# First mixer in held side stretches with its group scale applied behind the projection; loads and score banks reordered

## The chip, the cores and the metric

One core of one Trainium2 chip. The metric is device time in microseconds of one launch; the median of three timed runs of the kernel before is 1984.05 us.

## What is computed

A decoder trunk of two layers over 256 tokens of width 1024, all in float32. Each layer is a token mixer, a layer norm, a channel mixer that looks up experts by product keys (PEER), a layer norm, and a gated embedding. Layer 0's token mixer is Mamba-2 (SSD), layer 1's is causal attention with ALiBi over 16 heads (its block of 256 holds the whole sequence). The change touches both token mixers and nothing of PEER. Cut to what matters:

```python
# layer 0: SSD, 4 groups of 8 heads of 64, state 128, two chunks of 128 tokens
z, xbc, dt = split(x @ w_in);  xbc = silu(causal_depthwise_conv(xbc, conv_w, conv_b))
cb = einsum('bclgn,bcsgn->bclsg', c_in, b_in)
y_diag = einsum('bclsgr,bcsgrp->bclgrp', cb[..., None] * decay_ls, x_dt)
states = einsum('bclgn,bclgr,bclgrp->bcgrpn', b_in, decay_to_end, x_dt)
y_off = einsum('bclgn,cbgrpn,bclgr->bclgrp', c_in, prev, exp(a_cum))
gated = (y_diag + y_off + d_skip * xs).reshape(.., G, 512) * silu(z).reshape(.., G, 512)
gated = gated * rsqrt(mean(square(gated), axis=-1) + LN_EPS)     # one scale per token and group
mix = (gated.reshape(.., 2048) * norm_g) @ w_out
# layer 1: attention
q, k, v = x @ w_qkv;  logits = q @ k * Dh**-0.5 - slope * distance (causal)
mix = (softmax(logits) @ v) @ w_out
# each layer, then
x = layer_norm(alpha * x + mix);  ffn = peer_ffn(x)
x = layer_norm(alpha * x + ffn);  x = x + sigmoid(x @ ple_w_gate) * (p @ ple_w_proj)
```

## The kernel before

A tile framework orders each engine's instructions when it builds the program: by program order where inputs are ready by its own estimate, so that later work may be put ahead of earlier work that it expects to wait. `issue_after` (`self.after`) puts what is traced inside behind a given instruction of the same engine. Each engine runs its instructions in that fixed order; SP issues all weight loads in order too.

Weights come in chunks of 128x1024 float32 (512 KB). `chunk` (L116) loads one into a ring of four raw buffers; `split` (L112) makes a high half on ScalarE (L113) and the low remainder on VectorE (L114), into a ring of four; TensorE then does three products per pair of operands (`mm3`, L136: high by high, high by low, low by high). `stationary` (L140) takes a chunk as weights, 24 matmuls of 256 columns into a `mm` bank; `moving` (L153) takes it as the moving operand, 6 matmuls of 512 columns into one of four `acc` banks. All other matmuls, the side work, are plain float32 and use the two `aux` banks.

`weave(main, side)` (L38) calls the main steps in order and spreads the side steps evenly behind them; side steps go behind the load and split of the main step's chunk.

First mixer, `ssd` (L244). For each of four groups: `ssd_in` (six chunks, each with a convolution of three VectorE steps, L361), `ssd_z` (four chunks), then the scan of `ssd_mix` as side work, then `ssd_norm`, and `ssd_out` (four chunks of the output projection). The order: in 0, in 1, z 0 and 1, in 2 and out 0, in 3 and z 2, z 3, out 1, out 2, out 3 with `end_mixer`.

`ssd_mix` (L423) has ten steps: `bc` (L433), `inputs` for two token chunks (transposes of x, L444), `weights` (L439), `carry` (B is turned, L454, copied by ScalarE, L456, multiplied to the state, L458, copied, L460), and `heads` for four pairs, each 12 records of 64-column matmuls in its own `aux` bank (L472, L474) and an eviction on VectorE (L475). `ssd_norm` (L481) gates y by z (L487), squares it (ScalarE) and sums it (GpSimd, L494), sums over partitions on TensorE (L499), takes the root (L503), puts the scale on a diagonal (L506), spreads it by a matmul with ones (L512), multiplies y by gain and scale (L520) and splits it into high and low. All four groups' products accumulate in the same four `acc` banks until the layer norm adds them to 2**0.5 x (`ln_sums`, L182).

`end_mixer` (L220) does the last chunks, the layer norm and the projection of p (`project`), whose weights `ple_load` (L210) has loaded and split.

Second mixer, `moba` (L545): eight steps j over pairs of heads. `meet` does the probabilities by v of pair j-1 (L614) and the scores of pair j+1 (L621) into both `aux` banks; `softmax` evicts each of four score blocks (L590) and takes its maximum (L592), then exponentials (L597) and the normalisation (L602); `turns` transposes pair j's probabilities (L640) into the same two banks. `ple_load` for this layer stands at j == 6.

## Time and profile before

| | us |
|---|---|
| median of 3 runs | 1984.05 (1983.73 to 1985.16) |
| the profiled execution | 1985.01 |
| its span, first to last instruction | 1983.2 |
| TensorE busy | 1965.4 |
| VectorE busy | 1548.0 |
| ScalarE busy | 1134.8 |
| GpSimd busy | 129.5 |

Durations in rows are those of the profiled execution. "Idle before" is the time in which an engine did nothing ahead of an instruction, with what released it. PE is TensorE's matmuls, PEld its weight loads, DVE VectorE, ACT ScalarE, POOL GpSimd. A float32 matmul stands as two records. Records overlap a little, since instructions are pipelined.

### The profile page before, as it was taken

The page shows a single profiled execution, that of the slowest core. Times are in us where ns is not written, and L with a number is a line of the kernel's source. Part 1 is how long each engine was busy: PE and PEld are TensorE (multiplying, and loading weights), DVE is VectorE, ACT ScalarE, POOL GpSimd, SP SyncE. Part 2 cuts the span into 40 slices and gives each one's busy share as a digit, 9 for nine tenths or more (in the row PEclk, how much of TensorE's full clock was granted, in tenths as well). Part 3 has the DMA queues.
Part 4 walks back from the last instruction along what each step waited for, and adds up shares of the span by engine and source line. Part 5 has one row for each costly group of instructions (what it writes and reads, how often), then busy time and mean ns, then how long its engine had stood idle before and what let it go on. Part 6 is the DMA issues. An engine that isn't in the chain of part 4 may idle for free.

```text
span 1983.2 us, 33753 instructions
## 1 busy us (share of the span) xinstructions
PE 1965.4 (99%) x12658; PEld 1692.4 (85%) x12658; DVE 1548.0 (78%) x3044; ACT 1134.8 (57%) x1920; POOL 129.5 (7%) x156
## 2 busy tenths in 40 slices
PE   8999999999999999999999999999999999999999
PEld 8988998888888888888888899888888888888887
DVE  8787559998888998866766755899888899886675
ACT  6755456677656444455536655667755654445553
POOL 0001001111111000000000000111111100000000
PEclk9999999999999999999999999999999999999999
DMA  7446668888787545666745556888878764566671
GB/s 285 161 139 222 208 181 237 225 215 247 213 218 213 187 162 180 229 215 203 247 135 175 197 195 182 231 226 220 244 214 221 211 190 164 175 226 218 203 249 66
DMA packets 121155, 403.01 MB, mean 203 GB/s; under 512 B 13440, under 2 KB 14368, under 8 KB 119328
## 3 DMA queue, kind: packets, MB, share of 16 engines
q1 hardware_dynamic: 102560, 367.29, 56.7%
q0 software_dynamic: 18432, 33.56, 9.9%
q8 instruction: 100, 1.64, 0.3%
q14 instruction: 63, 0.52, 0.1%
HBM read 360.92 MB, written 6.32 MB: 185 GB/s over the span
## 4 chain that ended last, share of the span: by engine, by line
PE 90%; DVE 5%; ACT 3%; issue 1%; DMA 1%; POOL 0%; SPq 0%; ACTq 0%; DVEq 0%; POOLq 0%
PE acc L138 41%; PE acc L149 22%; PE acc L150 11%; PE mm L138 10%; PE aux L895 3%; DVE hl L114 2%; ACT hl L113 1%; PE aux L743 1%; PE mm L388 1%; PE aux L472 0%; DVE act L779 0%; DVE act L780 0%; PE mm L173 0%; DMA raw<-in_w_xbc 0%; DVE act L782 0%
## 5 line engine op out<-in xcount | busy, mean ns | idle before, releaser
L114 DVE TENSOR_TENSOR hl<-raw,hl 128x1024 fp32r<-128x1024 f32 x626 | 760.8, 1221 | 245.6 <-ACT hl L113 244.1
L149 PE MATMUL acc<-xT,hl 128*128 128x512 f32 x2048 | 722.9, 397 | 0.0
L138 PE MATMUL acc<-hl,w 128*128 128x512 f32 x3024 | 695.4, 390 | 0.0
L113 ACT CAST hl<-raw 128x1024 fp32r<-128x1024 f32 x626 | 658.3, 1054 | 36.3 <-PE acc L138 15.8
L138 PEld LDWEIGHTS acc<-hl,w 128*128 128x128 f32 x3024 | 565.1, 188 | 116.7
L150 PE MATMUL acc<-xT,hl 128*128 128x256 f32 x2048 | 573.3, 280 | 0.4 <-DVE hl L114 0.4
L149 PEld LDWEIGHTS acc<-xT,hl 128*128 128x128 f32 x2048 | 384.4, 188 | 89.8
L150 PEld LDWEIGHTS acc<-xT,hl 128*128 128x128 f32 x2048 | 386.5, 189 | 1.1 <-DVE hl L114 1.1
L113 ACT CAST w<-act 128x256 fp32r<-128x256 f32 x252 | 102.2, 407 | 344.6 <-PE acc L138 344.6
L138 PE MATMUL mm<-xT,hl 128*128 128x256 f32 x1968 | 252.7, 286 | 1.9 <-DVE hl L114 0.8
L138 PEld LDWEIGHTS mm<-xT,hl 128*128 128x128 f32 x1968 | 240.3, 191 | 7.9 <-issue 4.0
L861 ACT COPY act<-acc 128x256 f32<-128x256 f32 x256 | 96.3, 376 | 254.5 <-PE acc L150 254.5
L114 DVE TENSOR_TENSOR w<-act,w 128x256 fp32r<-128x256 f32 x252 | 106.8, 424 | 78.6 <-ACT w L113 78.4
L865 POOL DMA_DIRECT2D act<-low x128 | 111.1, 868 | 758.8 <-ACT low L862 629.6
L902 DVE SCALAR_TENSOR_TENSOR act<-aux,act 128x256 f32<-128x256 f32 x256 | 90.7, 417 | 9.9 <-PE aux L895 9.9
L862 ACT COPY low<-acc 128x256 f32<-128x256 f32 x256 | 98.1, 383 | 0.0
L886 DVE TENSOR_TENSOR a<-oh,r 128x512 f16<-128x512 f16 x256 | 96.6, 419 | 0.0
L880 DVE TENSOR_TENSOR oh<-iota,r 128x1024 f16<-128x1024 f16 x128 | 87.6, 684 | 0.0
L895 PEld LDWEIGHTS <-oh 128*128 128x128 f16 x2048 | 63.3, 98 | 13.4 <-issue 13.4
L895 PE MATMUL aux<-a,oh 128*128 128x64 f16 x2048 | 70.9, 193 | 0.0
L852 ACT ACTIVATE act<-act 128x1024 f32<-128x1024 f32 x64 | 69.0, 1078 | 0.8 <-DMA act<-low 0.8
L197 POOL TENSOR_TENSOR ln_s<-ln_s,mhalf 128x1 f32<-128x1 f32 x8 | 4.4, 548 | 898.0 <-DVE ln_s L196 763.5
(214 smaller groups left out, 1276.6 us busy)
## 6 DMA issues: line engine op xcount, KB each, us to landing
raw<-in_u SPq DMA_DIRECT2D x256, 512.0 KB, 4.3
raw<-in_v SPq DMA_DIRECT2D x256, 512.0 KB, 4.3
act<-low POOLq DMA_DIRECT2D x128, 256.0 KB, 5.5
raw<-in_w_q SPq DMA_DIRECT2D x32, 512.0 KB, 4.1
raw<-in_w_xbc SPq DMA_DIRECT2D x24, 512.0 KB, 4.3
raw<-in_w_z SPq DMA_DIRECT2D x16, 512.0 KB, 3.3
raw<-in_w_so SPq DMA_DIRECT2D x16, 512.0 KB, 3.8
raw<-in_w_pg SPq DMA_DIRECT2D x16, 512.0 KB, 4.7
```

The source lines that it names most:

```text
L113: a = self.nc.scalar.copy(hi, src)
L114: b = self.nc.vector.tensor_tensor(lo, src, hi.bitcast(F32), op=OP.subtract)
L138: self.last_mm = self.nc.tensor.matmul(out, lhs(a), rhs(b), start=start and i == 0, stop=stop and i == 2).ins
L149: self.nc.tensor.matmul(o, hl[:, 0, c], self.xT[:, :, k, :], start=k == 0, stop=False)
L150: self.nc.tensor.matmul(out[:, :T], hl[:, 1, c], self.xT[:, 0, k, :], start=False, stop=k == KD - 1)
L861: nc.scalar.copy(act[e // 32][:, e % 32, :], pe[:, :T])
L862: copied = nc.scalar.copy(cur["low"][:, e % 2, :], pe[:, T:]).ins
L865: nc.gpsimd.dma_start(both, cur["low"], accum_op=OP.add)
L880: nc.vector.tensor_tensor(pairs(oh2), every(self.iota, P), twins(i2T, P), op=OP.is_equal)
L886: nc.vector.tensor_tensor(pairs(a2[:, k]), pairs(oh1), twins(g2[:, k], 64), op=OP.mult)
L895: nc.tensor.matmul(pg[:, t, :], oh2[:, t], a2[:, k, t], start=k == 0, stop=k == 1)
L902: nc.vector.scalar_tensor_tensor(v, pg[:, :, 32 * a:32 * a + 32].rearrange("p t e -> p e t"), 2.0 ** -12, v, op0=OP.mult, op1=OP.mult)
```

## The change

In the first mixer, the scan's steps per group become `enter` (C by B, B turned, sums of squares of the group before, first token chunk of x turned), `weights`, a pause, `carry` (state, second token chunk turned), `weights`, `decayed`, a pause, and `heads` with all four pairs in the two `aux` banks. The matmuls of each of these three side stretches are put behind the last weight matmul issued. The group's scale is no longer spread: y times gain is split at the gate, each group has its own accumulation in the `acc` banks, and VectorE adds the result times the scale (one value per partition) to x, which is loaded during out 0 and scaled by ScalarE. For the last group the layer norm's addition does it. Group 3's scan moves from z 3 to out 1, and the loads of gain and shift and of the per-layer weights move from out 2 and behind it to z 3. `pr` is allotted in `end_mixer`.

In the second mixer, the four score evictions stand ahead of the four maxima, `ple_load` stands at j == 1, and the first scores stand behind the whole of query 1's chunk.

```diff
-    def ln_sums(self, tb, acc, x, dump, pool):
+    def ln_sums(self, tb, acc, x, dump, pool, scales=None):
...
-            nc.vector.scalar_tensor_tensor(v, v, ALPHA, acc[h], op0=OP.mult, op1=OP.add, accum_out=sm[:, h:h + 1])
+            a, scale, b = (v, ALPHA, acc[h]) if scales is None else (acc[h], scales[:, tb:tb + 1], v)
+            nc.vector.scalar_tensor_tensor(v, a, scale, b, op0=OP.mult, op1=OP.add, accum_out=sm[:, h:h + 1])
...
-        self.pr = pool.tile([P, 2, D], F32, tag="ac", bufs=4, name="pr")
...
-                self.moving(accs[tb][h], hl, lhs(kp, tb), False, final)
+                first = scales is not None and not any(h == q[0] for q in last[:n])
+                self.moving(accs[tb][h], hl, lhs(kp, tb), first, final)
...
-        sums = [self.ln_sums(tb, accs[tb], x, dump, pool) for tb in range(2)]
+        sums = [self.ln_sums(tb, accs[tb], x, dump, pool, scales) for tb in range(2)]
...
+        self.pr = pool.tile([P, 2, D], F32, tag="ac", bufs=4, name="pr")
...
-            self.weave(zs[0] + zs[1], seg[2] + exp[:1] + seg[3] + ssm[0][:6] + exp[1:] + ssm[0][6:])
+            self.weave(zs[0] + zs[1], seg[2] + exp[:1] + seg[3] + ssm[0][:7] + exp[1:] + ssm[0][7:])
             self.ssd_silu(0)
             self.ssd_silu(1)
-            self.oacc = self.accs()
-            self.weave(ins[2] + out[0], norm[0] + ssm[1])
+            def load():
+                nc.sync.dma_start(x, dram["x"].rearrange("(b p) d -> p b d", p=P))
+                for tb in range(2):
+                    nc.scalar.activation(x[:, tb], x[:, tb], AF.Copy, scale=ALPHA)
+
+            def roots():
+                pq = self.aux()
...
+                    self.ssd_sums(3, pq)
...
+            self.weave(ins[2] + out[0], norm[0] + ssm[1][:4] + [load] + ssm[1][4:])
             self.weave(ins[3] + zs[2], norm[1] + ssm[2])
             self.ssd_silu(2)
-            self.weave(zs[3], ssm[3][:6])
+            gb = pool.tile([P, 2, D], F32, tag="ac", bufs=4, name="gb")
+            self.weave(zs[3], [lambda: self.load_gb(gb, 0), lambda: self.ple_load(0, pool)])
             self.ssd_silu(3)
-            load = lambda: nc.sync.dma_start(x, dram["x"].rearrange("(b p) d -> p b d", p=P))
-            self.weave(out[1], ssm[3][6:] + norm[2] + [load])
-            gb = pool.tile([P, 2, D], F32, tag="ac", bufs=4, name="gb")
-            self.weave(out[2], norm[3] + [lambda: self.load_gb(gb, 0)])
-            self.ple_load(0, pool)
+            self.weave(out[1], norm[2] + ssm[3])
+            self.weave(out[2], norm[3] + [roots])
             self.weave(out[3], [])
             dump = pool.tile([P, D], F32, tag="y", bufs=2, name="dump")
             self.end_mixer(0, self.oacc, x, gb, dump, pool, self.last,
-                           lambda kp, tb: lambda a, k: self.ns[kp // 2][:, a, 2 * (kp % 2) + k, tb * P:(tb + 1) * P])
+                           lambda kp, tb: lambda a, k: self.ns[3][:, a, 2 * kp + k, tb * P:(tb + 1) * P], self.rs[3])
...
+        def enter():
...
+            p, px = self.aux(), self.aux()
+            with self.after((self.last_mm,)):
+                for c in range(2):
+                    sl = slice(c * P, (c + 1) * P)
+                    nc.tensor.matmul(p[:, sl], v["bf"][:, sl], v["cf"][:, sl], start=True, stop=True)
+                nc.tensor.transpose(p[:, T:T + P], v["bf"][:, :P], self.ident)
+                if g:
+                    self.ssd_sums(g - 1, p[:, 384:388])
+                turn(px, 0)
+            if g:
+                self.ssd_root(g - 1, p[:, 384:388])
+            v["bn"] = self.tl([P, P], "bn", 1)
+            nc.scalar.copy(v["bn"], p[:, T:T + P])
+            v["xe"] = scaled(px, "xe", 1, self.dtd[:, hs, None])
+            v["x", 0] = scaled(px, "xd", 4, self.dt[:, 0, hs, None])
             v["cb"] = self.tl([P, 2, P], "cbm", 2)
...
-            pb = self.aux()
...
-            pst = self.aux()
-            nc.tensor.matmul(pst, bn, v["xe"].rearrange("p h q -> p (h q)"), start=True, stop=True)
+            px, pst = self.aux(), self.aux()
+            with self.after((self.last_mm,)):
+                nc.tensor.matmul(pst, v["bn"], v["xe"].rearrange("p h q -> p (h q)"), start=True, stop=True)
+                turn(px, 1)
+            v["x", 1] = scaled(px, "xd", 4, self.dt[:, 1, hs, None])
             v["st"] = self.tl([P, 512], "st", 2)
             nc.scalar.copy(v["st"], pst)
+
+        def decayed():
...
             ce = self.ce[g]
             nc.vector.tensor_tensor(ce, ce, v["cf"][:, None, P:].to_broadcast([P, 8, P]), op=OP.mult)
...
-        def heads(j):
...
-            py = self.aux()[:, :T].rearrange("p (c l) -> p c l", c=2)
...
+        def heads():
+            y = self.ys[g] = self.tl([P, 4, T], "y", 2)
+            py = [self.aux().rearrange("p (j c l) -> p j c l", j=2, c=2) for _ in range(2)]
+            lanes = lambda j: [(2 * j + k, py[j // 2][64 * k:64 * k + 64, j % 2]) for k in range(2)]
+            with self.after((self.last_mm,)):
+                for j in range(4):
+                    for c in range(2):
+                        for h, o in lanes(j):
+                            nc.tensor.matmul(o[:, c], v["x", c][:, h, :], self.ac[g][:, h, c, :], start=True, stop=c == 0)
+                    for h, o in lanes(j):
+                        nc.tensor.matmul(o[:, 1], v["st"][:, 64 * h:64 * h + 64], self.ce[g][:, h, :], start=False, stop=True)
+            for j in range(4):
+                nc.vector.scalar_tensor_tensor(y[:, j, :], v["xs"][:, j, :], prm[:, P_D + 4 * g + j:P_D + 4 * g + j + 1],
+                                               py[j // 2][:, j % 2].rearrange("p c l -> p (c l)"), op0=OP.mult, op1=OP.add)
+
+        return [enter, lambda: weights(0), None, carry, lambda: weights(1), decayed, None, heads]
...
+                self.ns[g] = self.tl([P, 2, 4, T], "nhl", 2, F32R)
+                self.sq[g] = self.tl([P, T], "sq", 2)
+                nc.scalar.activation(self.sq[g], y, AF.Square)
...
-                nc.gpsimd.tensor_tensor(v["sq"], v["sq"], t, op=OP.add)
...
-        def scale():
-            pq = self.aux()
-            for tb in range(2):
-                nc.tensor.matmul(pq[:, 2 * tb:2 * tb + 2], v["sq"][:, tb * P:(tb + 1) * P], self.ones[:, :2],
-                                 start=True, stop=True)
-            rs = self.tl([P, 2], "rs", 2)
-            nc.vector.tensor_scalar(rs, pq[:, 0:4:2], 1.0 / 512, LN_EPS, op0=OP.mult, op1=OP.add)
-            nc.gpsimd.tensor_tensor(rs, rs, self.mhalf, op=OP.pow)
-            dg = self.tl([P, 2, P], "dg", 1)
-            for tb in range(2):
-                nc.vector.tensor_scalar(dg[:, tb, :], self.ident, rs[:, tb:tb + 1], None, op0=OP.mult)
-            v["dg"] = dg
-
-        def spread():
-            pr = self.aux()
-            dg = v["dg"]
-            nc.tensor.matmul(pr[:, :T], self.ones, dg.rearrange("p b t -> p (b t)"), start=True, stop=True)
-            v["rs"] = self.tl([P, T], "rsb", 2)
-            nc.scalar.copy(v["rs"], pr[:, :T])
-            self.ns[g] = self.tl([P, 2, 4, T], "nhl", 2, F32R)
-
-        def apply(j):
-            y, n = self.ys[g][:, j, :], self.ns[g]
-            c = 4 * g + j
-            nc.vector.scalar_tensor_tensor(y, y, prm[:, P_NG + c:P_NG + c + 1], v["rs"], op0=OP.mult, op1=OP.mult)
-            self.split(n[:, 0, j, :], n[:, 1, j, :], y)
-
-        return [lambda j=j: gate(j) for j in range(4)] + [None, scale, spread] + [lambda j=j: apply(j) for j in range(4)]
-
-    def ssd_out(self, g):
+                nc.gpsimd.tensor_tensor(self.sq[g], self.sq[g], t, op=OP.add)
+            n, gain = self.ns[g], prm[:, P_NG + 4 * g + j:P_NG + 4 * g + j + 1]
+            hi = n[:, 0, j, :]
+            nc.scalar.activation(hi, y, AF.Identity, scale=gain)
+            nc.vector.scalar_tensor_tensor(n[:, 1, j, :], y, gain, hi.bitcast(F32), op0=OP.mult, op1=OP.subtract)
+
+        return [lambda j=j: gate(j) for j in range(4)]
...
+    def ssd_sums(self, g, pq):
+        for tb in range(2):
+            self.nc.tensor.matmul(pq[:, 2 * tb:2 * tb + 2], self.sq[g][:, tb * P:(tb + 1) * P], self.ones[:, :2],
+                                  start=True, stop=True)
...
+            if kp + h == 0:
+                self.oacc = self.accs()
...
-                self.last.append((h, 2 * g + kp, hl, (0, 1)))
+                self.last.append((h, kp, hl, (0, 1)))
...
             for tb in range(2):
-                self.moving(self.oacc[tb][h], hl,
-                            lambda a, k: self.ns[g][:, a, 2 * kp + k, tb * P:(tb + 1) * P], g == 0 and kp == 0, False)
+                acc = self.oacc[tb][h]
+                self.moving(acc, hl, lambda a, k: self.ns[g][:, a, 2 * kp + k, tb * P:(tb + 1) * P], kp == 0, kp == 1)
+                if kp:
+                    v = x[:, tb, h * 512:(h + 1) * 512]
+                    self.nc.vector.scalar_tensor_tensor(v, acc, self.rs[g][:, tb:tb + 1], v, op0=OP.mult, op1=OP.add)
...
-                        nc.vector.tensor_reduce(mx[:, h2, tb:tb + 1], lg[:, h2, tb, :w], AX, OP.max)
+                for h2 in range(2):
+                    for tb in range(2):
+                        nc.vector.tensor_reduce(mx[:, h2, tb:tb + 1], lg[:, h2, tb, :(tb + 1) * P], AX, OP.max)
...
-            met = meet(None, 0)
-            with self.after(met):
-                q(1)
+            q(1)
+            meet(None, 0)
...
-                if j == 6:
+                if j == 1:
                     self.ple_load(1, pool)
```

## Rows read from the trace of the kernel before

**Rows 1.** The page: engines' busy time, then costliest groups (busy, mean ns | idle before).
```profile
PE 1965.4 (99%) x12658; PEld 1692.4 (85%) x12658; DVE 1548.0 (78%) x3044; ACT 1134.8 (57%) x1920; POOL 129.5 (7%) x156
...
L114 DVE TENSOR_TENSOR hl<-raw,hl 128x1024 fp32r<-128x1024 f32 x626 | 760.8, 1221 | 245.6 <-ACT hl L113 244.1
...
L113 ACT CAST hl<-raw 128x1024 fp32r<-128x1024 f32 x626 | 658.3, 1054 | 36.3 <-PE acc L138 15.8
```
**Rows 2.** Table by stage: window, then us and count for PE, PEld, DVE, ACT, POOL, clock, DMA.
```profile
0.00:216.00 216.00, 207.22 (x1446) 181.61 (x1446) 171.48 (x349) 136.44 (x232) 15.11 (x22) 1.00 0.58 199
...
1025.00:1160.00 135.00, 131.00 (x886) 112.32 (x884) 86.38 (x180) 77.43 (x171) 1.08 (x2) 1.00 0.48 165
```
**Rows 3.** The same table on a finer grid, one stretch of the convolutions.
```profile
125.00:145.00 20.00, 19.89 (x166) 19.64 (x165) 19.12 (x36) 13.26 (x28) 0.71 (x1) 1.00 0.35 112
```
**Rows 4.** The chain that ended last, first mixer: start us, us, what.
```profile
92.45 0.43 PE aux L512 x2
...
147.45 1.02 PE mm L138 x7
...
148.84 2.10 PE mm L138 x16
...
156.73 2.88 PE mm L138 x24
```
**Rows 5.** TensorE's waits, 0 to 216 us: total, times, longest.
```profile
PE aux L474 <- ACT st L460: 1.1, 1, 1.1
...
PE aux L458 <- ACT bn L456: 0.8, 2, 0.6
...
PE aux L512 <- DVE dg L506: 0.7, 1, 0.7
```
**Rows 6.** VectorE's groups by form, 55 to 216 us.
```profile
L520 DVE SCALAR_TENSOR_TENSOR y<-y,params,rsb 128x256 f32<-128x256 f32 x16 | 7.3, 480 | 0.1
...
L114 DVE TENSOR_TENSOR nhl<-y,nhl 128x256 fp32r<-128x256 f32 x16 | 6.4, 420 | 0.0
...
L182 DVE SCALAR_TENSOR_TENSOR xn<-xn,acc 128x512 f32<-128x512 f32 x4 | 2.7, 686 | 2.0 <-PE acc L138 2.0
...
L506 DVE TENSOR_SCALAR dg<-ident,rs 128x128 f32<-128x128 f32 x8 | 2.1, 283 | 3.1 <-POOL rs L503 3.1
```
**Rows 7.** DMA issues by tile, 100 to 216 us: size, median us to landing.
```profile
xn<-in_x SPq DMA_DIRECT2D x1, 1024.0 KB, 7.3
...
gb<-in_ln SPq DMA_DIRECT2D x1, 1024.0 KB, 6.5
```
**Rows 8.** TensorE's waits, 990 to 1170 us.
```profile
PE aux L640 <- DVE lg L590: 2.6, 3, 1.1
...
PE aux L640 <- ACT pt L644: 0.6, 1, 0.6
...
PE aux L621 <- ACT k L575: 0.5, 1, 0.5
```
**Rows 9.** Timelines in the second mixer: VectorE, TensorE, ScalarE (start us, us).
```profile
1084.58 0.61 DVE L592 TENSOR_REDUCE mx<-lg 128x1 f32<-128x256 f32 x2
...
1085.10 0.41 DVE L590 SCALAR_TENSOR_TENSOR lg<-alibi,aux 128x256 f32<-128x256 f32 x1
...
1085.58 0.82 PE L640 MATMUL aux<-ident,lg 128*128 128x128 f32 x6
...
1114.08 0.62 ACT L113 CAST pT<-raw 128x512 fp32r<-128x512 f32 x1 [3.46 <-DMA raw<-in_pT]
...
1121.54 1.22 DVE L114 TENSOR_TENSOR ppw<-raw,ppw 128x1024 fp32r<-128x1024 f32 x1
...
1125.15 0.52 PE L640 MATMUL aux<-ident,lg 128*128 128x128 f32 x3 [0.95 <-DVE lg L590]
```
**Rows 10.** Timeline of GpSimd, first mixer, two of its sums of squares.
```profile
119.03 2.37 POOL L494 TENSOR_TENSOR sq<-sq,sqt 128x256 f32<-128x256 f32 x3 [28.35 <-ACT sqt L493]
...
164.97 3.36 POOL L494 TENSOR_TENSOR sq<-sq,sqt 128x256 f32<-128x256 f32 x3 [37.47 <-ACT sqt L493]
```

More of the change, by code (lines that the diff above doesn't have):

```diff
@@ L217, in ple_load, with end_mixer @@
         self.ppw = [self.chunk(self.dram["w_pp"][i, h], hl=tile()) for h in range(2)]
-        self.pr = pool.tile([P, 2, D], F32, tag="ac", bufs=4, name="pr")
-    def end_mixer(self, i, accs, x, gb, dump, pool, last, lhs):
+    def end_mixer(self, i, accs, x, gb, dump, pool, last, lhs, scales=None):
         for tb in range(2):
@@ L262, in ssd @@
             x = pool.tile([P, 2, D], F32, name="xn")
-            self.grp, self.zs, self.ns, self.ys, self.ac, self.ce = ({} for _ in range(6))
+            self.grp, self.zs, self.ns, self.ys, self.ac, self.ce, self.sq, self.rs = ({} for _ in range(8))
             self.last = []
@@ L268, in ssd @@
             norm = [self.ssd_norm(g) for g in range(4)]
-            out = [self.ssd_out(g) for g in range(4)]
+            out = [self.ssd_out(g, x) for g in range(4)]
             seg = [[lambda g=g, c=c, k=k: self.ssd_seg(g, c, slice(4 * k, 4 * k + 4)) for c in range(2) for k in range(2)]
@@ L478, in ssd_mix @@
-        return [bc, lambda: inputs(0), lambda: weights(0), lambda: inputs(1), lambda: weights(1), carry] + [
-            lambda j=j: heads(j) for j in range(4)]
+        def heads():
+            y = self.ys[g] = self.tl([P, 4, T], "y", 2)
+            py = [self.aux().rearrange("p (j c l) -> p j c l", j=2, c=2) for _ in range(2)]
+            lanes = lambda j: [(2 * j + k, py[j // 2][64 * k:64 * k + 64, j % 2]) for k in range(2)]
+            with self.after((self.last_mm,)):
+                for j in range(4):
[4 more added lines that the diff above has]
+                        nc.tensor.matmul(o[:, 1], v["st"][:, 64 * h:64 * h + 64], self.ce[g][:, h, :], start=False, stop=True)
+            for j in range(4):
+                nc.vector.scalar_tensor_tensor(y[:, j, :], v["xs"][:, j, :], prm[:, P_D + 4 * g + j:P_D + 4 * g + j + 1],
+                                               py[j // 2][:, j % 2].rearrange("p c l -> p (c l)"), op0=OP.mult, op1=OP.add)
@@ new lines, in ssd_norm, with ssd_root @@
+        return [lambda j=j: gate(j) for j in range(4)]
[3 more added lines that the diff above has]
+                                  start=True, stop=True)
+    def ssd_root(self, g, pq):
+        nc = self.nc
+        rs = self.rs[g] = self.tl([P, 2], "rs", 2)
+        nc.vector.tensor_scalar(rs, pq[:, 0:4:2], 1.0 / 512, LN_EPS, op0=OP.mult, op1=OP.add)
+        nc.gpsimd.tensor_tensor(rs, rs, self.mhalf, op=OP.pow)
```

43 lines of the change are left out of this document (10 added, 33 removed).

## The prediction

> **What bounds the kernel now.** I first read the page for the busiest engine. TensorE is busy for 1965.4 us, 99% of the span [rows 1], so only removed matmul time, or one of the few waits in front of a matmul, can move the end. Next I read the table by stage. The first mixer (0 to 216 us) leaves TensorE idle for 8.8 us and the second (1025 to 1160 us) for 4.0 us [rows 2]; the reader should see that these two hold 12.8 of the span's 17.8 us of TensorE idle time (part of it the first load of all), and they are what the change touches. The same table on a finer grid shows the second engine at risk: in 125 to 145 us VectorE is busy 19.12 of 20 us [rows 3], because it writes the low half of each weight chunk. A VectorE edit there is not free.
>
> The profiled execution took 1985.01 us, a span of 1983.2 and 1.8 around it. It is 1.0 us above the median of the three timed runs (1984.05), so I make the sum on 1985.01 and take 1.0 off at the end. A measurement of this kernel can tell about 0.2% (4 us) from no change.
>
> **Removed in the first mixer: the spread of the scale.** Before, each group's scale per token is put on a diagonal and multiplied by ones, to stand along the free axis, before the output projection. Now it is one number per partition that multiplies the projection's result. In the chain one spread holds TensorE for 0.43 us [rows 4], and there are four: 4 x 0.43 = 1.7 us, all on the path, as TensorE does nothing else meanwhile.
>
> **Removed there: waits that sit in front of side matmuls.** The table of TensorE's waits lists 1.1 us for the state copy (line 460), 0.8 us for the copy of turned B (line 456) and 0.7 us for the diagonal (line 506) [rows 5]: 2.6 us. The diagonal is gone. The copy of B is now made in `enter`, three steps ahead of `carry`, which reads it, and the state copy four steps ahead of `heads`; a step is a chunk of 2.9 us [rows 4] or longer. The cover is that distance. If ScalarE sits behind a late transfer, the old price returns. What is late next after these is the weight chunk itself, by VectorE's splits.
>
> **Removed there: breaks in a weight chunk.** Before, the first head pair of a group cut into a chunk of 24 matmuls. In group 2 its two pieces took 1.02 + 2.10 = 3.12 us, and an uncut chunk 2.88 us [rows 4]: 0.24 us lost. Groups 1 and 2 are cut like this, group 3 once: 2.5 x 0.24 = 0.6 us. In group 0 I count nothing: there the head pairs stand while ScalarE is still working off its exponentials, so the weight chunk behind them would not be ready earlier.
>
> **Added there.** VectorE loses 16 gain multiplications (0.48 us each), 16 low halves of 0.42 and 8 diagonals of 0.28 [rows 6], by mean durations 7.7 + 6.7 + 2.3 = 16.7 us. It gains 16 low halves with the gain in them (the nearest row is the gain multiplication, 0.48) and 12 evictions of 512 columns that scale and add (nearest, the layer norm's addition at 0.69) [rows 6]: 7.7 + 8.2 = 15.9 us. So VectorE's total hardly moves, but the place does. In the two stretches of convolutions it gets 2 x (16.7 - 7.7) / 4 = 4.5 us back and pays 4 x 0.69 = 2.8 us at the end of the first. For the evictions: behind one on VectorE stand weight splits, and TensorE behind those; the accumulation bank it frees is next needed three products of six matmuls later. Nothing I can see makes that late. ScalarE gains two scalings of x. A cast of the same size takes 1.05 us [rows 1], so 2.1 us, in a place where it waits for TensorE; behind them stand the state copy and weight casts. They wait for the load of x, which landed 7.3 us after its issue [rows 7]. It is issued with the chunk that many steps later reaches TensorE, so I cost it at nothing; uncovered, it would cost up to those 7.3 us once.
>
> **Moved there.** The gain and shift (1 MB, landed after 6.5 us [rows 7]) and the per-layer weights (three more transfers, three casts, three splits) go ahead of the second output projection, into the last z stretch; group 3's scan moves out of it. On the SP queue they now stand ahead of the first output chunk, and in the ring of four raw buffers they take three places. I work out the margin: the last z chunk can be split once the chunk four before it has left TensorE, about four chunks (11.5 us) ahead of the output chunk's need; a transfer as slow as that of the gain and shift (6.5 us [rows 7]), a cast of 1.05 and a split of 1.22 [rows 1] leave some 3 us. I cost it at nothing, and up to 3 us if the queues slip.
>
> **New waits of held stretches.** Each group now has three side stretches, each after the last matmul of the chunk: 12 in all, and none can be slipped under a late chunk. The sum of squares of group g-1 stands in the middle of group g's `enter`; if GpSimd is late, four transposes and the next chunk wait behind it. The trace of before has no held stretch. Bounds: nothing, since inputs are one or more chunks old, or the 1.1 us of the worst side wait [rows 5] each time, 13 us. I take 0.8 us in total, near the low end, because the waits of before hit steps whose input had been issued in the same or the neighbouring step, and only the sum of squares is still like that.
>
> First mixer: -1.7 - 2.6 - 0.6 + 0.8 = -4.1 us.
>
> **Second mixer.** The table of TensorE's waits around it lists 2.6 us in three waits of the turning step for score evictions (line 590), 0.6 for the probabilities' copy and 0.5 for the key's copy at the scores [rows 8]. The first two kinds stand from 1125 us on, where the per-layer weights are prepared: ScalarE had sat 3.46 us for their transfer, and VectorE put their split of 1.22 us between the weight splits and the score evictions [rows 9]. The turning step needs the two banks that those evictions empty. Moving the load from step 6 to step 1 removes that cluster, and the maxima no longer stand between the evictions (two of them held the last eviction from 1084.58 to 1085.10, 0.5 us [rows 9]): 2.6 + 0.6 = 3.2 us off. The same three casts and splits then land in the loop's first steps, where the last eviction ended 1085.51 and the transposes began 1085.58 [rows 9]: 0.07 us of slack. Their price there is between nothing and what they cost before (3.2); I take 0.7, nearer to the first, since a split of 1.22 less the 0.5 and what little slack there is leaves 0.6 to 0.7, and not each of the three need fall in that window. The first scores now come after the second half of their chunk. That can remove the 0.5 us wait or, if the key's copy falls behind the shifted exponentials, add up to 1.4 us (twelve matmuls of 0.12 us, from the uncut chunk); I take nothing. Second mixer: -3.2 + 0.7 = -2.5 us.
>
> **Sum.** 1985.01 - 4.1 - 2.5 = 1978.4, and 1.0 less for the median: **1977.4 us**. With all covers (0.8 and 0.7 not paid, 0.5 gained at the first scores, and up to 3 us from the room VectorE gets in the convolutions) it is 1972.5.
>
> **Rivals.** First, *the gain is absorbed*: TensorE reaches the next chunk sooner, but its low half is paced by VectorE (19.12 of 20 us), and in the second mixer the load only carries its waits along. For it: VectorE's row, the 0.07 us. Against it: VectorE gets room just there, and in the second mixer the waits stand beside a 3.46 us transfer wait that step 1 doesn't have. It leaves the spreads and some waits: 1984 - 2 = 1982. Chance 0.21.
>
> Second, *held stretches stall*, slower: TensorE waits at each of 12 stretches as it did at the worst one, 12 x 1.1 = 13 us, against a gain of 4.9 + 2.5 = 7.4 without them: 1984 + 6 = 1990. It decides from (7.4 + 4) / 12 = 0.95 us a stretch. For it: the sum of squares runs through VectorE, ScalarE and GpSimd with three serial additions. Against it: only the four sums depend on that, the other eight have whole chunks of lead. Chance 0.09.
>
> GpSimd's three additions took 2.37 us for group 1 and 3.36 us for group 2 [rows 10], with VectorE busy beside them. The Trainium skill (SBUF — State Buffer, section "SBUF: two separate sides") says that GpSimd and a VectorE instruction with two SBUF inputs share one port pair, and that whoever starts first locks the other out for a whole instruction. By that rule VectorE's splits could hold each addition for a whole split and make the held sums late; the longer row agrees in kind. I give this as the way into the second rival, with its chance.
>
> Worked from rows: three additions held by 1.22 us each are 3.7 us late, against a lead of one chunk of 2.9 us: 0.8 us for each of three groups, 2.4 us, so 1980.
>
> **How the numbers follow.** The forecast, a gain of 4 to 12 us, 0.70; absorbed, within 0.2%, 0.21; slower 0.09. The range of 1972.5 to 1984.0 takes in all covers on one side and the absorbed case on the other.
>
> **What would show it.** Line 512's matmuls gone; no wait of TensorE for the state copy or B's copy; one run of 48 head matmuls per group; the first mixer shorter by some 4 us and the second by 2 to 3; in the second mixer no TensorE wait for score evictions. Wrong would be: TensorE waiting for squares from GpSimd inside `enter`, or for weight splits at the start of an output chunk, or new waits at the turning steps of pairs 1 to 3.

## The result, and the profile after

The changed kernel takes **1972.77 us** (median; 1972.6 to 1973.5) where the kernel before, timed beside it, takes 1984.39 (1983.58 to 1985.52). The ratio is 0.9941, with a 95% interval of 0.9930 to 0.9953: faster by 11.6 us, 0.6%. I had forecast 1977.4 in a range of 1972.5 to 1984.0. The direction held and the time lies in the range, at its lower end: the gain is nearly twice the 7 us that I worked out, so most of what follows asks which terms were too small.

The first lines of the page of after, engines' busy time. VectorE's total hardly moved against [rows 1], and TensorE lost 6.2 us of busy time, so half of the gain isn't idle time at all.

```profile
span 1970.9 us, 33730 instructions
...
PE 1959.2 (99%) x12650; PEld 1691.9 (86%) x12650; DVE 1551.7 (79%) x3032; ACT 1135.9 (58%) x1918; POOL 133.4 (7%) x156
```

The table by stage of after, columns as in [rows 2]. TensorE's idle time in the first mixer fell from 8.8 to 6.2 us (4.6 of it the first load), in the second from 4.0 to 1.1. The third line is a stretch of convolutions, projection and scan: TensorE never stops there, and VectorE is busy 43.19 of 44 us (38.50 in the same 44 us of before, which hold slightly other work).

```profile
0.00:208.00 208.00, 201.84 (x1439) 180.87 (x1440) 175.64 (x337) 137.65 (x231) 19.03 (x22) 1.00 0.60 207
1017.00:1149.00 132.00, 130.88 (x889) 112.39 (x888) 86.50 (x180) 78.16 (x171) 1.08 (x2) 1.00 0.50 169
...
100.00:144.00 44.00, 44.00 (x347) 40.72 (x346) 43.19 (x65) 25.53 (x47) 3.67 (x4) 1.00 0.56 183
```

TensorE's waits of after, 50 to 210 us and then 980 to 1165 us (total, times, longest). Against [rows 5] and [rows 8], the waits for the state copy, for B's copy and for the diagonal are gone. In the second mixer 0.2 us of score evictions (line 605) is left of 2.6, and a wait of 0.2 for the normalised probabilities (line 619) is new.

```profile
PE mm L173 <- DVE xn L201: 0.8, 1, 0.8
...
PE mm L173 <- DVE x L201: 0.3, 1, 0.3
PE mm L138 <- DVE xT L114: 0.3, 1, 0.3
PE aux L657 <- DVE lg L605: 0.2, 1, 0.2
PE aux L657 <- DVE lg L619: 0.2, 1, 0.2
```

To say where a change lands, I use marks on TensorE's timeline that every kernel here has: the first matmul of z (47.3 us in before), the first query matmul of PEER behind the first mixer, the second mixer's first query matmul, and PEER's first query matmul behind that. From before to after the span shrank by 12.4 us: 8.61 between the first two marks, 3.25 in the second mixer, 0.58 in the PEER between them and 0.08 behind it, less 0.15 for a later first mark. The changed code touches the first two terms alone. The PEER stretch took 841.87 us in another execution of before, so its 0.58 is what single executions differ by, and so is a part of the second mixer's figure (below). The experiments, by these marks (us; idle is TensorE's in that stretch, and what is left of a stretch without it is called matmul time). Each ratio is to executions of before timed beside that kernel, whose medians were 1983.72 to 1984.39:

| kernel | median | ratio to before (95%) | first mixer (idle) | second mixer (idle) |
|---|---|---|---|---|
| before | 1984.39 | 1 | 168.99 (3.73) | 101.52 (4.29) |
| before, another execution (e9) | 1984.97 (one run) | | 169.11 (3.88) | 100.96 (3.75) |
| after | 1972.77 | 0.9941 (0.9930-0.9953) | 160.38 (0.81) | 98.27 (1.12) |
| e1, first mixer's edits only | 1975.35 | 0.9956 (0.9939-0.9972) | 160.38 (0.83) | 99.95 (2.91) |
| e2, scale only | 1977.54 | 0.9967 (0.9954-0.9979) | 163.04 (1.00) | 99.95 (2.94) |
| e3, held stretches only | 1981.77 | 0.9991 (0.9981-1.0000) | 165.74 (4.04) | 100.61 (3.37) |
| e4, after without lead | 1975.89 | 0.9960 (0.9946-0.9974) | 163.67 (1.95) | 98.28 (1.12) |
| e5, after, head pairs one by one | 1975.55 | 0.9959 (0.9945-0.9974) | 163.04 (1.24) | 98.26 (1.10) |
| e6, second mixer's load only | 1982.23 | 0.9993 (0.9984-1.0003) | 169.25 (4.03) | 99.53 (2.43) |
| e7, maxima only | 1982.47 | 0.9993 (0.9983-1.0002) | 168.56 (3.30) | 99.73 (2.56) |
| e8, first scores' place only | 1984.74 | 1.0004 (0.9995-1.0014) | 168.43 (3.16) | 100.55 (3.10) |
| e10, after, loads back | 1974.90 | 0.9955 (0.9937-0.9973) | 161.99 (2.26) | 98.26 (1.10) |
| e11, after, spread back | 1975.56 | 0.9958 (0.9943-0.9973) | 163.31 (2.15) | 98.27 (1.10) |
| e12, after, first chunk in halves | 1973.56 | 0.9948 (0.9930-0.9966) | 160.40 (0.84) | 98.26 (1.10) |

### The profile page after: what moved, and what is told of

It reads as the page before. It is cut to its first block, busy times and chain, and to the rows that moved or that the text cites. A ratio compares the mean times of both kernels' runs of the same rounds, so it can differ in the third digit from the quotient of the medians.

```text
span 1970.9 us, 33730 instructions
## 1 busy us (share of the span) xinstructions
PE 1959.2 (99%) x12650; PEld 1691.9 (86%) x12650; DVE 1551.7 (79%) x3032; ACT 1135.9 (58%) x1918; POOL 133.4 (7%) x156
## 4 chain that ended last, share of the span: by engine, by line
PE 94%; DVE 4%; ACT 1%; issue 1%; DMA 0%; SPq 0%; POOL 0%; ACTq 0%; DVEq 0%
PE acc L138 42%; PE acc L149 22%; PE mm L138 12%; PE acc L150 11%; PE aux L911 3%; DVE hl L114 1%; PE mm L399 1%; PE aux L759 1%; ACT hl L113 1%; PE aux L494 0%; PE mm L173 0%; DVE act L795 0%; DVE act L796 0%; DMA raw<-in_w_xbc 0%; PE aux L631 0%
```

## The experiments

**Which mixer.** e1 is after with the second mixer's three edits undone.

```diff
-                if j == 1:
+                if j == 6:
                     self.ple_load(1, pool)
-            q(1)
-            meet(None, 0)
+            met = meet(None, 0)
+            with self.after(met):
+                q(1)
```

(and the maxima back between the evictions.)

> The first mixer as changed, the second as before. First mixer = span start to the first matmul of PEER's queries (216.3 us before, 207.9 after). If the two mixers are independent: first mixer 207.9 us, second unchanged, 1984.4 - 8.5 = 1976 us. Rival, that part of the second mixer's gain is only a shifted pattern of the first's: first mixer 207.9, second shorter than before by 1 us or more.

Its median is 8.7 us under the before timed beside it (1984.08) and 2.6 above after's, and its first mixer is as long as after's to 0.01 us. So the first mixer gave some three quarters of the gain. Its second mixer, written as in before, took 99.95 us, 1.0 to 1.6 less than in the two executions of before: the rival's sign is there. Whether that is a pattern shifted by the first mixer, or what single executions differ by, stays open. By the marks, then, the second mixer's edits are worth 1.7 us between e1 and after (99.95 against 98.27), not the whole 3.25. The rest of the 2.6 shows in these two executions ahead of the first mark and in the last PEER stretch, which no edit touches.

**Which half of the first mixer's edit.** e2 has the ten old scan steps, with the scale applied behind the projection: no spread, gain in the low half, each group its own accumulation, x loaded and scaled early. The moved loads are at their old places. e3 has the opposite: the new scan in held stretches, with the old norm, the diagonal and the spread.

```diff
# e2, against before
-        return [gate ...] + [None, scale, spread] + [apply ...]
+        return [gate ...] + [None, scale]
# e3, against before
-        return [bc, inputs(0), weights(0), inputs(1), weights(1), carry] + [heads(0) ... heads(3)]
+        return [enter, weights(0), None, carry, weights(1), decayed, None, heads]
```

> Only the group scale on the projection's result (own accumulation per group, x loaded and scaled early, sums of squares as a step of their own, spread and diagonal gone); the scan's steps and all else as before. Additive theory: 1.7 us of spreads, 0.7 of the diagonal's wait and some 1 us from VectorE's room, first mixer 212.5 to 213.5 us, 1981 us. Rival, the scale edit is the larger part through VectorE's pace: 210.5 us or less. Rival, the old scan's waits for B and the state absorb it: 214.5 us or more.

> Only the held stretches of the scan (enter, carry, heads), with the old spread, diagonal and single accumulation. Additive theory: 1.9 us of waits for the state and for B, 1 to 2 us of breaks, first mixer 212.5 to 213.5 us, no wait for the state or B copy left, 1981 us. Rival, that the stretches gain only when the scale leaves VectorE and the banks: 214.5 us or more.

The scale alone took 5.95 us off the first mixer, the stretches alone 3.25, and both together 8.61: nearly a sum. The scale's part is larger than I expected: by the expectation's measure, from the span's start, e2's first mixer took 210.1 us, inside the first rival's bound, and e3's 212.9, as expected. By e3's times alone, whose interval reaches 1, it can't be told from before. Of e2's 5.95 us, 2.73 is idle time and 3.22 matmul time; e3 lost 3.56 of matmul time and gained 0.31 of idle. The two matmul figures make 6.78 where after lost 5.69, so they overlap: in e2 the framework's order no longer cuts the first head pairs of groups 1 and 2, although the scan's steps are the old ones. TensorE's waits between 50 and 220 us, to be read beside [rows 5], first of e2, then of e3:

```profile
PE mm L173 <- DVE xn L201: 0.8, 1, 0.8
PE aux L464 <- ACT bn L462: 0.2, 1, 0.2
```

```profile
PE aux L519 <- DVE dg L513: 3.1, 3, 2.0
...
```

e2 has no wait for the state copy, though its scan is the old one. Its order shows why, beside that of before. Here are VectorE and then ScalarE of before around the state copy (start us, us; brackets: idle before, and its releaser):

```profile
106.74 1.22 DVE L462 TENSOR_TENSOR ce<-ce,cf 128x1024 f32<-128x1024 f32 x1
107.88 3.49 DVE L114 TENSOR_TENSOR hl<-raw,hl 128x1024 fp32r<-128x1024 f32 x3
```

```profile
111.46 1.05 ACT L113 CAST hl<-raw 128x1024 fp32r<-128x1024 f32 x1 [5.04 <-DVE hl L114]
112.42 0.58 ACT L460 COPY st<-aux 128x512 f32<-128x512 f32 x1
```

and ScalarE of e2:

```profile
107.34 0.59 ACT L466 COPY st<-aux 128x512 f32<-128x512 f32 x1 [1.22 <-PE aux L464]
```

In before, the state's matmuls were issued at 108.72, yet the copy began at 112.42: a cast stood ahead of it in ScalarE's queue, which waited 5.04 us for VectorE, and VectorE was working off three splits behind the scan's multiplications. In e2 the copy waits only for its own matmul. So this wait for the state (group 1's) is VectorE's backlog, handed on through ScalarE's queue; a step's distance to its reader is one way around it and less work at that place is the other. In e3 the diagonal, still on VectorE and still read a step later, became the late one: 3.1 us in three waits.

**What the lead is worth.** e4 is after with the stretches held in the same places but each issued as late as it can be.

```diff
-        return [enter, lambda: weights(0), None, carry, lambda: weights(1), decayed, None, heads]
+        return [enter, lambda: weights(0), None, None, None, None, None,
+                lambda: [f() for f in (carry, lambda: weights(1), decayed, heads)]]
```

> The changed kernel with carry, second weights, decayed and heads all in the last step, so that what heads reads is made one step ahead at most. If the lead of the inputs is what hides the stretches: breaks in the next chunk and waits of up to 1.1 us per group come back, first mixer 209.5 to 212 us, 1975 to 1977 us. Rival, that the framework's order covers a late input by itself: within 0.5 us of the changed kernel's 207.9 us.

The first mixer grew by 3.29 us, of which 1.14 is idle. A wait for a sum of squares appears, 0.6 us, the only one of that kind in any kernel here, and one for a weight chunk's high half:

```profile
...
PE aux L526 <- POOL sq L516: 0.6, 1, 0.6
PE mm L138 <- ACT hl L113: 0.4, 1, 0.4
```

The other 2.15 us is matmul time: the framework had put weight matmuls between the late heads, and in groups 1, 2 and 3 they cut into the first head pairs again, as in before. The lead buys unbroken runs more than it buys waits.

**What a break costs.** e5 is after with the four head pairs as four steps again, in the same two banks, with `enter` and `carry` as early as in after.

```diff
-        return [enter, lambda: weights(0), None, carry, lambda: weights(1), decayed, None, heads]
+        return [enter, lambda: weights(0), None, carry, lambda: weights(1), decayed] + [lambda j=j: heads(j) for j in range(4)]
```

> The changed kernel with the four head pairs of a group as four steps again (same banks, same inputs, same early carry), so that weight chunks stand between most of them: about two more breaks per group. If breaks are the large term that was under-counted (about 3 us in the first mixer instead of 0.6): first mixer 1.5 to 3 us longer than the changed kernel's, with no new idle gaps of TensorE. Rival, that breaks are worth only what the cut chunk shows (0.24 us per group): 0.5 to 1 us longer.

The first mixer grew by 2.66 us: 0.43 idle, for the low half of one weight chunk, which the expectation had not foreseen, and 2.23 of matmul time with the same matmuls. TensorE's timeline of e5 in group 2 (start us, us, records):

```profile
141.15 0.66 PE L498 MATMUL aux<-ac,xd 128*64 128x128 f32 x8
141.63 0.39 PE L500 MATMUL aux<-ce,st 128*64 128x128 f32 x4
141.95 3.14 PE L138 MATMUL mm<-xT,hl 128*128 128x256 f32 x24
145.02 0.66 PE L498 MATMUL aux<-ac,xd 128*64 128x128 f32 x8
```

From one head pair to the next with a whole chunk between them it is 3.87 us. The chunk alone is 2.88 [rows 4], and a pair inside a run is 0.65 to 0.71 (after's timeline, below), so such a break costs 0.28 to 0.34 us. From the end of group 1's heads to the end of group 2's, over the same work, e5 takes 35.09 us and after 34.40: 0.35 for each of two breaks. e5's order has five breaks more than after's: these two, two in group 1 at 0.48 each (without the idle time) and one in group 0 at 0.58, together the 2.23.

**What a spread costs.** e11 is after with one matmul by ones, of the spread's size, in each group's `enter`; nothing reads its result.

```diff
+            pr = self.aux()
+            with self.after((self.last_mm,)):
+                nc.tensor.matmul(pr[:, :T], self.ones, v["xs"][:, 0, :], start=True, stop=True)
```

> The changed kernel with one dead matmul of the spread's size (ones by 128x256, two records) per group behind enter. If the price read from the chain holds: 4 x 0.43 = 1.7 us longer in the first mixer, 1974.5 us. Rival, that a matmul next to other float32 side work costs only its own 0.25 us: 1 us.

The first mixer grew by 2.93 us, of which 1.34 is idle, since the extra bank waits for an eviction:

```profile
PE aux L461 <- DVE xd L445: 1.3, 1, 1.3
...
```

The remaining 1.59 is 0.40 for each spread, beside the 0.43 that [rows 4] shows. It is a net figure: in e11 the heads of group 3 stand in one run, which in after they don't (below), and that gave back 0.35. The four matmuls themselves took 0.43, 0.65, 0.42 and 0.43 us. In groups 0 to 2 the order put them between weight matmuls, where the spread stood in before, and not beside the side work of `enter`, so the rival is not tested there.

**The moved loads.** e10 is after with gain and shift loaded in the third output projection and the per-layer weights behind it, where before has them.

```diff
-            self.weave(zs[3], [lambda: self.load_gb(gb, 0), lambda: self.ple_load(0, pool)])
+            self.weave(zs[3], [])
...
-            self.weave(out[2], norm[3] + [roots])
+            self.weave(out[2], norm[3] + [lambda: self.load_gb(gb, 0), roots])
+            self.ple_load(0, pool)
```

> The changed kernel with the gain and shift and the per-layer weights loaded in out 2 and behind it again. Prediction's view, that their place costs nothing either way in the first mixer: within 0.5 us of 1972.8 us. Rival, that the last z stretch was bought by this move: 1 us or more longer, with waits for weight splits in out 2 or out 3.

It is 2.1 us slower than after by the medians and 2.4 by the spans. Between the marks of the first mixer it lost 1.6 us, 1.45 of it idle; the rest lies in the PEER stretch behind, which is the same code (843.19 us, the longest here). TensorE's waits at the end of the mixer:

```profile
PE mm L173 <- DVE xn L201: 1.5, 1, 1.5
PE mm L138 <- DVE xT L114: 0.7, 1, 0.7
```

against a single one of 0.8 in after. They are waits for the layer norm and for the split of its transposes, not for weight splits in the output projection as the rival had it. TensorE's order differs too: e10 does six of the projection's 24 matmuls (1.4 us) ahead of the last output chunks, so that the layer norm's additions start 1.4 us later (194.10 against 192.66) and fewer matmuls are left to fill its wait. The old place of the loads does not bring these waits by itself: e2 has it, with group 3's scan still begun in z 3, and waits 0.8 us there as after does. So the move of the loads is worth about 1.6 us once that scan stands in out 1; the two moves were not tried apart. The intervals of e10 and after overlap; the two waits are the firmer evidence.

**The second mixer's edits one by one**, each alone in the kernel before: e6 moves the load, e7 the maxima, e8 the first scores.

```diff
# e6
-                if j == 6:
+                if j == 1:
# e7
-                        nc.vector.tensor_reduce(mx[:, h2, tb:tb + 1], lg[:, h2, tb, :w], AX, OP.max)
+                for h2 in range(2):
+                    for tb in range(2):
+                        nc.vector.tensor_reduce(mx[:, h2, tb:tb + 1], lg[:, h2, tb, :(tb + 1) * P], AX, OP.max)
# e8
-            met = meet(None, 0)
-            with self.after(met):
-                q(1)
+            q(1)
+            meet(None, 0)
```

> Kernel before, only the second mixer's per-layer weights moved from step 6 to step 1. Second mixer = first matmul of its query 0 to its last transposes (100.95 us before, 97.71 changed). If the cluster of casts and splits makes the waits at 1125 and 1135 us: 98.0 to 98.8 us, 1981.5 us. Rival, the load carries its waits along: 100 us or more.

> Kernel before, only the maxima behind the four evictions. If the banks' release is what the transposes wait for: 0.5 us off each of two waits, second mixer 99.9 to 100.3 us, 1983.3 us. Rival, that it does all of it alone: 98.5 us.

> Kernel before, only the first scores behind the whole of query 1. If the key's copy then goes ahead of the exponentials: its 0.53 us wait is gone, second mixer 100.4 us. Rival: the copy falls behind the later exponentials, 101.5 to 102.4 us.

By their times none of the three can be told from before. By the marks e6 is 1.4 to 2.0 us shorter in the second mixer than the two executions of before, e7 1.2 to 1.8, e8 0.4 to 1.0. But e1, e2 and e3, whose second mixer is written as in before, took 99.95, 99.95 and 100.61 us there, so the marks alone don't show that these gains are the edits'. The expectations end the second mixer at its last transposes, 0.57 us ahead of my mark; by that measure e6 took 99.0 us, e7 99.2 and e8 100.0: the load a little less of a gain than expected, the other two somewhat more. The waits say more. TensorE's waits from 1040 us on, of e6, then e7, then e8:

```profile
PE aux L621 <- ACT k L575: 0.8, 2, 0.5
PE aux L640 <- ACT pt L644: 0.6, 1, 0.6
PE aux L640 <- DVE lg L590: 0.4, 2, 0.2
...
```

```profile
PE aux L642 <- DVE lg L590: 1.4, 2, 0.7
PE aux L623 <- ACT k L575: 0.5, 1, 0.5
...
```

```profile
PE aux L640 <- DVE lg L590: 1.6, 2, 1.1
PE aux L640 <- ACT pt L644: 0.6, 1, 0.6
...
PE aux L640 <- DVE lg L602: 0.2, 1, 0.2
```

Two waits go with one edit each, in every kernel here. The 0.53 us for the key's copy at the first scores stands wherever these have their old place and nowhere else; in its stead comes 0.17 for the normalised probabilities (line 602). The 0.57 for the probabilities' copy stands wherever the maxima stand between the evictions and nowhere else, so it is the maxima that end it, not the load. Of the score evictions the load's move leaves 0.4 of 2.6 us, and it adds two small waits in the early steps, 0.25 for the key's copy and 0.24 of that 0.4. The maxima alone leave 1.4. The two attack the same waits, so their gains don't add. How much of each is the edit's can't be said closer: e1 has 1.1 us of score waits, where two executions of before have 2.6 and (e9)

```profile
PE aux L640 <- DVE lg L590: 2.0, 3, 1.1
...
```

I had expected of e9 that the five waits of before's second mixer would return within 0.1 us. Four did. One score wait was 0.95 us [rows 9] in one execution and 0.42 in the other, and is absent in e1, e2, e3 and e8.

**A first chunk in halves.** In after the first thing that TensorE waits for, behind the input, is the first weight chunk's split (0.8 us). e12 loads and splits that chunk in two parts.

```diff
-            self.first = self.chunk(dram["w_xbc"][16])
+            self.first = self.chunk(dram["w_xbc"][16], parts=2)
```

> The changed kernel with the very first weight chunk loaded and split in two halves, since TensorE's largest wait left is the start. If the split of the whole chunk is what the first matmul of the first chunk waits for: its start 1.0 to 1.5 us earlier, 1971.5 us. Rival, that two transfers land later than one: no gain, 1972.8 us.

No gain: the first chunk runs without a wait, but TensorE waits 1.0 us at the chunk behind it, and both mixers are unchanged. No kernel tried here beats after.

## Why the prediction was right, and which terms were mis-sized

**Waits of the first mixer: right in size, wrong in part of the cause.** I took 2.6 us off for three waits [rows 5]. TensorE's idle time between the marks fell by 2.92. The other 0.3 is a wait of before that I had not counted, ahead of PEER's first query; after has none there:

```profile
...
PE mm L138 <- DVE xT L114: 0.3, 1, 0.3
```

I put the end of the waits for both copies down to distance alone; e2 shows that less work on VectorE ends the state's as well, with the old distance between the steps as they are written. The size is less firm than it looks: the state's wait was 1.12 us in one execution of before, 1.33 in the other, and 1.4, 0.7 and 0.6 in e6, e7 and e8, whose first mixer is written as in before.

**Spreads: right.** 1.7 us predicted, 1.6 net and 1.9 for the four matmuls themselves by e11.

**Breaks: the mis-sized term.** I took 0.6 us. TensorE's matmul time between the marks fell by 5.69 us (168.99 - 3.73 against 160.38 - 0.81); less 1.6 for the spreads, 4.1 is left, seven times my figure. e3, which keeps the spreads, needs no such subtraction: it lost 3.56 us of matmul time (168.99 - 3.73 against 165.74 - 4.04). TensorE's timeline of group 2's heads, before and then after:

```profile
146.79 0.66 PE L472 MATMUL aux<-ac,xd 128*64 128x128 f32 x8
147.38 1.09 PE L138 MATMUL mm<-xT,hl 128*128 128x256 f32 x7
148.40 0.44 PE L474 MATMUL aux<-ce,st 128*64 128x128 f32 x4
148.77 2.17 PE L138 MATMUL mm<-xT,hl 128*128 128x256 f32 x16
150.88 0.66 PE L472 MATMUL aux<-ac,xd 128*64 128x128 f32 x8
...
153.14 1.10 PE L138 MATMUL mm<-xT,hl 128*128 128x256 f32 x7
```

```profile
144.87 0.66 PE L494 MATMUL aux<-ac,xd 128*64 128x128 f32 x8
145.36 0.39 PE L496 MATMUL aux<-ce,st 128*64 128x128 f32 x4
145.58 0.61 PE L494 MATMUL aux<-ac,xd 128*64 128x128 f32 x8
...
147.32 0.39 PE L496 MATMUL aux<-ce,st 128*64 128x128 f32 x4
147.64 3.62 PE L138 MATMUL mm<-xT,hl 128*128 128x256 f32 x28
```

Before, the heads with a chunk cut into them took 153.14 - 146.79 = 6.35 us; less the chunk's 2.88 they cost 3.47. After, the same 48 records in one run take 147.64 - 144.87 = 2.77. The chunk's pieces were 0.24 us longer than the whole, as I had read; the other 0.46 was in the heads themselves, and I didn't look there. About 0.3 of it lies in the first two pairs, beside the cuts, and 0.15 where the third pair meets the fourth. No chunk stands between these two; in before each pair has a bank of its own, so the price need not be all of the cuts. The same reading gives 0.81 us for group 0, about 0.9 for group 1 and 0.70 for group 2. In group 3 it gives only some 0.15, because there a weight matmul stands in the heads of after too:

```profile
173.26 0.66 PE L494 MATMUL aux<-ac,xd 128*64 128x128 f32 x8
173.85 0.50 PE L138 MATMUL acc<-hl,nhl 128*128 128x512 f32 x1
...
```

So the sign that I named, one run of 48 head matmuls per group, holds in three groups of four. The four groups make 2.6 us. That includes group 0, which I had counted at nothing: its weight chunks were ready, and its heads gained as the others did. e5 confirms the cause by putting breaks back in the same two banks. The other 1.5 of the 4.1 us I ascribe to the scan's other side work, which in before stands in five places per group (groups 1 and 2) and in after in two; no run takes that apart.

**New waits of held stretches: 0.8 taken, none found.** No wait for a sum, a copy or a scaled x stands in after. The rival in which the stretches stall falls. Where I looked for danger, the sums of squares, TensorE waited only without lead: 0.6 us, once, in e4. But in group 0 of after it was close. Here are GpSimd's last addition and TensorE's matmul that reads it:

```profile
89.48 1.47 POOL L516 TENSOR_TENSOR sq<-sq,sqt 128x256 f32<-128x256 f32 x1 [3.66 <-ACT sqt L515]
```

```profile
91.27 0.51 PE L526 MATMUL aux<-ones,sq 128*128 128x2 f32 x4
```

The sum was ready at 90.95, 0.3 us ahead; in the other groups the lead was 2.5 us or more. So that group 0 paid nothing is in part luck. Whether the holding itself does anything is not shown: no run leaves the holds out and keeps the places of the steps. It does not keep a stretch whole by itself, since in e4, and in group 3 of after, weight matmuls stand inside held heads.

**The sums under VectorE's splits.** GpSimd's additions took 1040 ns on average after against 836 before. Two additions from GpSimd's timeline of after, and then the instructions of VectorE that ran beside them, a split beside the first and a step of a convolution that began just behind the second:

```profile
82.62 1.54 POOL L516 TENSOR_TENSOR sq<-sq,sqt 128x256 f32<-128x256 f32 x1 [82.17 <-ACT sqt L515]
...
119.81 0.74 POOL L516 TENSOR_TENSOR sq<-sq,sqt 128x256 f32<-128x256 f32 x1 [1.27 <-ACT sqt L515]
```

```profile
82.00 1.22 DVE L114 TENSOR_TENSOR hl<-raw,hl 128x1024 fp32r<-128x1024 f32 x1
...
119.86 0.96 DVE L379 SCALAR_TENSOR_TENSOR cv_y<-cv_raw,params,cv_y 128x254 f32<-128x254 f32 x1
```

The Trainium skill (SBUF — State Buffer, section "SBUF: two separate sides") has GpSimd and a VectorE instruction with two SBUF inputs lock each other out for a whole instruction, whichever starts first. The trace agrees in kind, both ways round: the addition that began inside a split took 1.54 us against 0.74, and the convolution step that began behind an addition took 0.96 against 0.47 elsewhere. The rival that I built on it, sums 0.8 us late in three groups, did not happen: no wait of TensorE for GpSimd is in after.

**VectorE's exchange: neither its price nor its place was right.** I priced the low halves at 0.48 us and the evictions at 0.69. VectorE's groups by form, 55 to 216 us of after (busy, mean ns):

```profile
L520 DVE SCALAR_TENSOR_TENSOR nhl<-y,params,nhl 128x256 fp32r<-128x256 f32 x16 | 10.9, 694 | 0.5 <-ACT nhl L519 0.4
...
L548 DVE SCALAR_TENSOR_TENSOR xn<-acc,rs,xn 128x512 f32<-128x512 f32 x12 | 8.6, 744 | 0.2 <-PE acc L138 0.2
```

Together 19.5 us where I added 15.9, so that VectorE has 3.7 us more in the whole kernel instead of 0.8 less. Most of it is in the low halves: the eight of the sixteen that began while an addition of GpSimd ran took 0.67 to 0.97 us, the other eight 0.47 to 0.49. I also expected room on VectorE in the convolutions, up to 3 us of gain. It is fuller there: from the end of group 0's heads to the end of group 1's, over the same work of TensorE, it was busy 31.57 of 36.81 us before and all of 34.14 us after. That cost nothing, since TensorE never stopped in that stretch, but it leaves no slack in it.

**Moved loads: costed at nothing, worth about 1.6 us beside the other moves.** Only a loss stood in my bounds. e10 shows the gain: without the move, TensorE waits 1.5 and 0.7 us at the layer norm and at the first query instead of 0.8. In the sum this shows less, since before has these two waits at 0.7 and 0.3, and e2, with the loads where before has them, at 0.8 and none.

**Second mixer: right in sum, not in each part.** I predicted 2.5 us. Found are 2.7 and 3.25 against the two executions of before, and 1.7 against e1, which differs from after in these edits alone. The score evictions' waits, 2.6 us in before, fell to 0.2. The probabilities' 0.6, which I had put with the load's cluster, stays when the load alone moves (e6) and ends with the maxima (e7). The key's 0.5, for which I took nothing between -0.5 and +1.4, ended with the first scores' new place, at the price of 0.17. The price of the load in early steps, taken as 0.7, is 0.5 in e6 (0.25 for the key's copy at 1081 us, 0.24 for a score eviction at 1085.6) and nothing in after, whose one early wait (0.17 at 1068) e8 has too, without the load's move.

**The rival of the absorbed gain** fell as well: it needed VectorE to pace TensorE, and TensorE stood still for 0.81 us in all between the first mixer's marks. Its ground was sound only in that VectorE is nearly full.

**The sum again**, with what was measured: -1.6 spreads, -2.9 waits, -4.1 breaks and fewer pieces, -1.7 to -3.25 in the second mixer, which makes 10.3 to 11.9 against 11.6 by the medians. The breaks' figure is what the other terms leave of the first mixer, so the sum can't fail there. Had the breaks stood in my sum at 4.1 and the new waits at 0, the forecast would have been 1973.1. That the measured time lies in the range at all is in part luck: the lower end (1972.5; my terms add up to 1972.4), 0.3 us below it, was reached by 3 us of room on VectorE that didn't come, and 3.5 us of breaks that I had not counted stood in for them.

## What to carry to other kernels

On an engine that is 99% busy, look for the gain in the busy time: compare the same small matmuls in a run and cut apart, on both sides of each cut, before pricing only the waits. A wait for a short copy often belongs to what is queued ahead of that copy; taking work off the engine that blocks the queue and issuing the copy earlier are two cures for one ill, and they don't add. A load that costs nothing at its place can cost there once other work moves beside it: e2 and e10 have the same place, and e10 alone pays.

## What the runs showed of the hardware that I had not expected

Changing between the head matmuls (float32, weights of 64 columns, 128 columns moved past them) and a weight chunk (256 or 512 columns moved) cost 0.35 to 0.58 us of TensorE time a break in e5, where the chunk was whole, and 0.70 us in group 2 of before, where it was cut in two, with the granted clock at 1.00 throughout and no wait recorded for it. A two-input instruction of VectorE on 128x256 elements took 473 to 970 ns for the same form and size in one kernel, the long ones all beside GpSimd's additions. And single waits of an unchanged piece of a program moved by half a microsecond between executions (0.95 and 0.42 us for the same score wait), which is why second-mixer edits of 0.5 to 2 us could be seen in the waits, but hardly by the marks and not in a median.
